# Other scratch tiles for the top-k masks, other banks and places for the index-query evictions, split first loads, and a later load of the last norm's scale, in a hybrid decoder layer

## The chip, the cores and the metric

One core of a Trainium2 chip. The time is that of one execution on the device, in microseconds. Engines are named as in the profile: PE (TensorE) with its weight loads PEld, DVE (VectorE), ACT (ScalarE), POOL (GpSimd) and SP (SyncE, which here only issues loads). The kernel before takes 1724.82 us (median of three runs, 1723.39 to 1730.63).

## The reference

One decoder layer for 1024 tokens of width 1024, all in float32:

```python
proj = x @ w_in                                  # 4696 columns: z, xbc, dt, q, k, v, qi, ki, wi
xbc  = silu(causal_conv4(xbc))                   # 1536 channels
y    = ssd_scan(xs, dt, a, bm, cm) + d_skip * xs # 16 heads x 64, 8 chunks of 128
y_ssd = rms_norm_by_group(y * silu(z)) * ssd_norm_g
ki   = layer_norm(ki)                            # one index key of 64 per token
score = sum_h wi_h * relu(qi_h . ki / 8)         # 8 index heads; causal
keys  = top_k(score, 256)                        # per query
y_att = softmax(q . k / 8 over keys) @ v         # 16 heads, 4 kv heads
h    = layer_norm(2**0.25 * x + [y_ssd, y_att] @ w_out)
u    = causal_conv3(h @ w_up)                    # 2 x 2816 columns
out  = layer_norm(2**0.25 * h + (silu(gate) * up) @ w_down)   # ln2_g, ln2_b
```

## The kernel before, in words

Matmuls run in a float32 form in which each operand is split into a high and a low part; `three` (lines 157 to 160) makes one product of three matmuls. A weight tile is loaded to `w_raw`, split by ACT or POOL to `w_hi` and by POOL or DVE to `w_lo`.

The work in order of the program: `x` is loaded in eight blocks of 128 tokens and turned by PE (`xtp`) to `xTh`, `xTl`, in two halves of 512 tokens; a small projection gives dt, the index key and its weights, and the key is normed on DVE (`kn`, `kih`, `kil`). Four index-query tiles follow (lines 441 to 453): each is two halves of 24 matmuls into a bank, and of each half ACT copies two quarters and DVE makes the two low parts. Then the scores of blocks 7 to 2, each the sum of eight heads (PE, a relu by ACT, an accumulation by DVE), are woven with the first projections. Blocks 0 and 1 need no search.

The search for each query's 256th largest score (`topk_gen`) sets one bit of a threshold in each of 32 rounds, by counts on DVE (blocks 6, 4, 3) and ACT (7, 5, 2). After it, `topk_gen` makes one mask for each of the six blocks, all on DVE: `eq`, `pen` and `cum` are its scratch tiles (lines 379 to 411). Beside the search and the masks runs the generator `main`: the convolutions (`conv_tile`, raw rows in `xbc`), the SSD scan of two head groups, chunk by chunk (`ssd_gen`), their gates (`gate_gen`), the projections of z, v and q, and the key loads of attention (`k_load`). Two steps of `topk_gen` go with five of `main`. Attention (`att_unit`), the output projection, the first norm, the up-projection, and the down-projection in seven products P1, P2, P6, P7, P4, P5, P3 follow. The last norm uses `g2`, `b2`, loaded as two broadcast rows (`ln_consts`).

What sets the order: a planner lays out each engine's instructions at build time, by a simulated time line, taking those that come first in the program first; `tc.high_priority(n)` moves an instruction n places ahead. SP keeps the order of the program. A load that has to wait for a buffer so holds up every load behind it. Each buffer belongs to a group with a number of buffers, and a tile waits until one of its group is free. Those of this change, in SBUF: `s2` 5 (2 KB a partition: parts of the scan and the gates, `eq`, and at the start `crow`), `wo` 8 (4 KB: blocks of `x`, then scores, convolved rows, `pen`, `cum`, and the attention keys `kh`, `kl`), `tx` 4 (4 KB: raw rows of the convolutions), `t4` 18, `wr` 3 (raw loads: weights, and the attention keys `kraw`); in PSUM: `ip` 2, `lg` 3, `tp` 2, `pv` 1 banks.

Of the kernel before, what the change touches and what calls it, by code (L numbers as in the profile page):

```python
# [8 lines left out]
F32 = mybir.dt.float32  # L9
F32R = mybir.dt.float32r  # L10
BF16 = mybir.dt.bfloat16
I32 = mybir.dt.int32
AF = mybir.ActivationFunctionType
OP = mybir.AluOpType
# [43 lines left out]
def hybrid_layer(ctx, tc, x, w_in, ssd_conv_w, ssd_conv_b, dt_bias, a_log, d_skip, ssd_norm_g,  # L58
# [30 lines left out]
    def f(t):  # L89
        return t.bitcast(F32)  # L90
# [3 lines left out]


    xb = [big("xload", tag="wo") for _ in range(NB)]
    for b in range(4):
        nc.sync.dma_start(xb[b], x[b * P:(b + 1) * P, :])

    ident = consts.tile([P, P], F32, name="ident")  # L100
    make_identity(nc, ident)
# [87 lines left out]
    nc.sync.dma_start(crow[0:48], bass.AP(tensor=ssd_conv_w.tensor, offset=ssd_conv_w.offset, ap=[[P, 48], [1, P]]))  # L189
    nc.sync.dma_start(crow[48:60], bass.AP(tensor=ssd_conv_b.tensor, offset=ssd_conv_b.offset, ap=[[P, 12], [1, P]]))  # L190
    nc.sync.dma_start(crow[60:68], bass.AP(tensor=ssd_norm_g.tensor, offset=ssd_norm_g.offset, ap=[[P, 8], [1, P]]))
    cw = consts.tile([P, 68], F32, name="cw")
    ps = bank("cwps", "tp")
    nc.tensor.transpose(ps[:, :68], crow[:68], ident[:68, :68])
    nc.scalar.activation(cw, ps[:, :68], AF.Copy)

    for half in range(2):
        s = slice(half * 512, half * 512 + 512)
        for k in range(NK):
# [122 lines left out]
    def topk_gen():  # L322
        thr, val, cand = [], [], []
        for e, ch in enumerate(CHAINS):
            thr.append(consts.tile([P, len(ch)], F32, name=f"thr{e}"))
            val.append(consts.tile([P, len(ch)], F32, name=f"val{e}"))
            for i, (b, eng) in enumerate(ch):
                nc.vector.memset(thr[e][:, i:i + 1], float((b + 1) * P - (TOPK if eng == "dve" else 2 * TOPK)))
            cand.append(small(f"cand{e}", (P, len(ch)), I32))
            nc.vector.memset(cand[e], 0)  # L330
        junk = big("junk", BF16, (P, 2, 1024))
        junk = [junk[:, 0], junk[:, 1]]
        top, at, tile16 = {}, 2048, None
        for b in [b for ch in CHAINS for b, eng in ch if eng == "dve"]:
            n = (b + 1) * P
            if tile16 is None:
                tile16, at = big("top16", BF16, (P, 2048)), 0
            if at + n > 2048:
                continue
            top[b] = tile16[:, at:at + n]  # L340
            at += n
            halves = score_ap[b].bitcast(BF16).rearrange("p (n t) -> p n t", t=2)
            nc.vector.tensor_copy(top[b], halves[:, :, 1])
        for k in range(31, -1, -1):
            for e, ch in enumerate(CHAINS):
                shape = (P, len(ch))
                for i, (b, eng) in enumerate(ch):
                    n = (b + 1) * P
                    c = f(cand[e][:, i:i + 1])
                    if eng == "dve":  # L350
                        nc.vector.tensor_scalar(junk[0][:, :n], top[b] if k >= 16 and b in top else score_ap[b], c, None,
                                                op0=OP.is_lt, op1=OP.add, accum_out=val[e][:, i:i + 1])
                    else:
                        nc.scalar.activation(junk[1][:, :n], score_ap[b], AF.Sign, bias=c, scale=-1.0,  # L354
                                             accum_out=val[e][:, i:i + 1])
                base = cand[e]
                if 0 < k < 31:
                    base = small(f"base{e}", shape, I32)
                    nc.vector.tensor_scalar(base, cand[e], 1 << (k - 1), None, op0=OP.bitwise_xor)
                fail = small(f"fail{e}", shape, I32)  # L360
                nc.vector.tensor_tensor(fail, val[e], thr[e], op=OP.is_gt)
                new = small(f"cand{e}", shape, I32)
                if k == 31:
                    neg = small(f"neg{e}", shape, I32, bufs=1)
                    nc.vector.tensor_scalar(neg, fail, 31, 31, op0=OP.logical_shift_left, op1=OP.arith_shift_right)
                    nc.vector.tensor_scalar(new, neg, 1 << 30, None, op0=OP.bitwise_xor)
                else:
                    nc.vector.scalar_tensor_tensor(new, fail, k, base, op0=OP.logical_shift_left, op1=OP.bitwise_xor)  # L368
                cand[e] = new
            yield  # L370
        m76 = big("mask76", BF16, (P, 2048))
        m5 = big("mask542", BF16, (P, 2048))
        m3 = consts.tile([P, 512], BF16, name="mask3")
        mask_ap[7], mask_ap[6] = m76[:, :1024], m76[:, 1024:1920]
        mask_ap[5], mask_ap[4], mask_ap[2] = m5[:, :768], m5[:, 768:1408], m5[:, 1408:1792]
        mask_ap[3] = m3[:, :512]
        zero = consts.tile([P, 1], F32, name="zero1")
        nc.vector.memset(zero, 0.0)
        for e, ch in enumerate(CHAINS):
            for i, (b, eng) in enumerate(ch):  # L380
                n = (b + 1) * P
                sc = score_ap[b]
                v = f(cand[e][:, i:i + 1])
                eq = mid("eq", BF16, (P, 1024))
                if eng == "act":
                    t = v
                    cnt = small("cnt", (P, 3))
                    nc.vector.tensor_scalar(eq[:, :n], sc, t, None, op0=OP.is_gt, op1=OP.add,
                                            accum_out=cnt[:, 0:1])
                    pen = big("pen", tag="wo")  # L390
                    nc.vector.tensor_scalar(pen[:, :n], sc, t, 3.0e38, op0=OP.is_le, op1=OP.mult)
                    nc.vector.tensor_tensor_reduce(pen[:, :n], sc, pen[:, :n], 1.0, 3.0e38, OP.add, OP.min,
                                                   cnt[:, 1:2])
                    nc.vector.tensor_scalar(cnt[:, 2:3], cnt[:, 0:1], float(TOPK), None, op0=OP.is_ge)
                    nc.vector.tensor_scalar(cnt[:, 2:3], cnt[:, 2:3], 6.0e38 / 2, None, op0=OP.mult)
                    nc.vector.tensor_scalar(cnt[:, 0:1], cnt[:, 0:1], float(TOPK) - 0.5, None, op0=OP.is_lt)
                    nc.vector.tensor_scalar(cnt[:, 0:1], cnt[:, 0:1], -3.0e38, None, op0=OP.mult)
                    nc.vector.tensor_tensor(cnt[:, 2:3], cnt[:, 2:3], cnt[:, 0:1], op=OP.add)
                    v = small("vsel", (P, 1))
                    nc.vector.tensor_tensor(v, cnt[:, 1:2], cnt[:, 2:3], op=OP.min)  # L400
                    nc.vector.tensor_tensor(v, v, t, op=OP.max)
                    yield
                room = small("room", (P, 2))
                nc.vector.tensor_scalar(eq[:, :n], sc, v, None, op0=OP.is_gt, op1=OP.add, accum_out=room[:, 0:1])
                nc.vector.tensor_scalar(room[:, 1:2], room[:, 0:1], float(TOPK), -BIG, op0=OP.subtract, op1=OP.mult)
                nc.vector.tensor_scalar(eq[:, :n], sc, v, BIG, op0=OP.is_equal, op1=OP.mult)
                cum = big("cum", tag="wo")
                nc.vector.tensor_tensor_scan(cum[:, :n], eq[:, :n], zero.to_broadcast([P, n]), 0.0, OP.add, OP.add)
                nc.vector.scalar_tensor_tensor(eq[:, :n], cum[:, :n], room[:, 1:2], eq[:, :n], op0=OP.is_le, op1=OP.mult)
                nc.vector.tensor_scalar(eq[:, :n], eq[:, :n], -1.0, BIG, op0=OP.mult, op1=OP.add)  # L410
                nc.vector.scalar_tensor_tensor(mask_ap[b], sc, v, eq[:, :n], op0=OP.is_le, op1=OP.mult)
                yield
# [30 lines left out]
    for t in range(4):  # L443
        w = w_qi if t == 0 else next_w()
        a, c = big("qsa", F32R, tag="pp"), big("qsb", F32R, tag="pp")
        for half in range(2):
            s = slice(half * 512, half * 512 + 512)
            ps = cols_half(w, xt, half)
            nc.scalar.activation(a[:64, s], ps[:64], AF.Copy)
            nc.scalar.activation(c[64:, s], ps[64:], AF.Copy)  # L450
            nc.vector.tensor_tensor(a[64:, s], ps[:64], f(a[:64, s]), op=OP.subtract)
            nc.vector.tensor_tensor(c[:64, s], ps[64:], f(c[64:, s]), op=OP.subtract)  # L452
        qs += [a, c]


    def qk_tile(dst, t, halves=(0, 1), w=None):
# [632 lines left out]


    KT = NF // 2
    g2, b2 = ln_consts(ln2_g, ln2_b)

    def two(src, r0, step, c0, n, width, k, tag):

        m = min(2, KT - k)
# [115 lines left out]
        now(nc.scalar.activation, c1[t], pa[t], AF.Copy)  # L1212
    r1 = h_rows(0)
    run("P2", pa, True)
    for t in range(4):
        now(nc.vector.scalar_tensor_tensor, r1[t][:, N1], r1[t][:, N1], ALPHA, pa[t], op0=OP.mult, op1=OP.add)
        stats(st8[t], 0, r1[t])
# [53 lines left out]
```

## Time and profile before

| what | value |
|---|---|
| median of 3 runs | 1724.82 us |
| profiled execution | 1727.09 us, its span 1725.4 us |
| mean granted PE clock | 0.963 |
| busy PE / DVE / ACT / POOL | 1598.4 / 1212.8 / 921.4 / 873.9 us |
| moved by DMA | 232.86 MB, 135 GB/s in the mean |

The span runs from the first to the last instruction of the profiled execution. Busy time counts an engine's instructions; of PE it says nothing of its clock, which is told as a share of full speed: 1.00 is 2.4 GHz, 0.50 is 1.2 GHz, and a value between them is a stretch with both.

### The profile page before, as it was taken

The page shows a single profiled execution, that of the slowest core. Times are in us where ns is not written, and L with a number is a line of the kernel's source. Part 1 is how long each engine was busy: PE and PEld are TensorE (multiplying, and loading weights), DVE is VectorE, ACT ScalarE, POOL GpSimd, SP SyncE. Part 2 cuts the span into 40 slices and gives each one's busy share as a digit, 9 for nine tenths or more (in the row PEclk, how much of TensorE's full clock was granted, in tenths as well). Part 3 has the DMA queues.
Part 4 walks back from the last instruction along what each step waited for, and adds up shares of the span by engine and source line. Part 5 has one row for each costly group of instructions (what it writes and reads, how often), then busy time and mean ns, then how long its engine had stood idle before and what let it go on. Part 6 is the DMA issues. An engine that isn't in the chain of part 4 may idle for free.

```text
span 1725.4 us, 23252 instructions
## 1 busy us (share of the span) xinstructions
PE 1598.4 (93%) x7844; PEld 1322.7 (77%) x7844; DVE 1212.8 (70%) x2274; ACT 921.4 (53%) x1761; POOL 873.9 (51%) x659
## 2 busy tenths in 40 slices
PE   8899998987998779999999893999999999989997
PEld 6688887776888657778888772878888888768886
DVE  3533779899369377787787479677777678746468
ACT  3333597687642376666676444555555555442241
POOL 2222235544264353545474456667777676565480
PEclk9999998999999989999999996999999999989999
DMA  5122022132433473544454542233444333788782
GB/s 170 41 78 68 25 95 77 50 103 69 129 99 92 135 227 100 153 138 139 130 157 157 159 155 77 86 116 131 144 132 143 116 116 110 242 318 300 233 280 110
DMA packets 208271, 232.86 MB, mean 135 GB/s; under 512 B 13987, under 2 KB 138263, under 8 KB 208151
## 3 DMA queue, kind: packets, MB, share of 16 engines
q1 hardware_dynamic: 160423, 159.79, 30.9%
q10 hardware_dynamic: 47728, 71.58, 11.4%
q8 instruction: 62, 1.02, 0.3%
q14 instruction: 58, 0.48, 0.1%
HBM read 159.70 MB, written 71.63 MB: 134 GB/s over the span
## 4 chain that ended last, share of the span: by engine, by line
PE 52%; DVE 6%; DMA 2%; ACT 2%; issue 1%; POOL 1%; ACTq 0%; DVEq 0%; SPq 0%; POOLq 0%
PE acc L158 4%; PE acc L159 4%; PE acc L160 4%; PE ops L158 3%; PE ops L159 3%; PE ops L160 3%; PE ptp L690 3%; PE pa L158 2%; PE pa L160 2%; PE pa L159 2%; PE pc L160 2%; PE pc L158 2%; PE pc L159 2%; PE pd L158 2%; PE pd L160 2%; PE pd L159 2%
## 5 line engine op out<-in xcount | busy, mean ns | idle before, releaser
L158 PE MATMUL proj<-xTh,w_hi 128*128 128x512 f32 (+1 forms) x432 | 174.5, 404 | 17.3 <-DVE qsb L452 6.3
L160 PE MATMUL proj<-xTh,w_lo 128*128 128x512 f32 (+1 forms) x432 | 172.9, 401 | 2.8 <-POOL w_lo L131 2.8
L159 PE MATMUL proj<-xTl,w_hi 128*128 128x512 f32 (+1 forms) x432 | 174.6, 404 | 0.0
L684 POOL TENSOR_SCALAR prob<-prob,sm 128x512 f32<-128x512 f32 (+7 forms) x128 | 97.0, 768 | 138.4 <-DVE sm L683 108.2
L997 POOL TENSOR_TENSOR w_hl<-s,w_hl 128x512 fp32r<-128x512 f32 x88 | 120.0, 1371 | 58.2 <-ACT w_hl L996 54.2
L128 POOL TENSOR_SCALAR w_hi<-w_raw 128x1024 fp32r<-128x1024 f32 x35 | 39.6, 1133 | 172.2 <-PE proj L159 125.3
L131 POOL TENSOR_TENSOR w_lo<-w_raw,w_hi 128x1024 fp32r<-128x1024 f32 (+1 forms) x45 | 113.3, 2521 | 26.1 <-ACT w_hi L130 23.9
L159 PE MATMUL acc<-wd_hl,g_hl 128*128 128x512 f32 x308 | 121.1, 395 | 0.4 <-POOL wd_hl L1158 0.4
L160 PE MATMUL acc<-wd_hl,g_hl 128*128 128x512 f32 x308 | 120.9, 394 | 0.0
L997 POOL TENSOR_TENSOR w_hl<-w_raw,w_hl 128x512 fp32r<-128x512 f32 x66 | 91.0, 1381 | 58.7 <-ACT w_hl L996 56.6
L158 PE MATMUL acc<-wd_hl,g_hl 128*128 128x512 f32 x308 | 110.9, 395 | 9.2 <-ACT wd_hl L1157 9.2
L681 ACT ACTIVATE prob<-prob,mx 128x512 f32<-128x512 f32 (+7 forms) x128 | 98.5, 771 | 36.5 <-DVE mx L678 36.3
L692 ACT ACTIVATE pt<-ptp 128x512 fp32r<-128x512 f32 x144 | 81.1, 595 | 64.6 <-PE ptp L690 43.9
L158 PEld LDWEIGHTS proj<-xTh,w_hi 128*128 128x128 f32 (+1 forms) x432 | 82.8, 192 | 37.5 <-issue 7.1
L1158 POOL TENSOR_TENSOR wd_hl<-keep,wd_hl 128x512 fp32r<-128x512 f32 x55 | 82.5, 1526 | 53.5 <-ACT wd_hl L1157 47.0
L158 PE MATMUL ops<-w_hi,y_hi 128*128 128x512 f32 x256 | 104.5, 408 | 3.1 <-ACT y_hi L130 3.1
L693 DVE TENSOR_TENSOR pt<-ptp,pt 128x512 fp32r<-128x512 f32 x144 | 95.4, 684 | 15.4 <-ACT pt L692 15.1
L159 PE MATMUL ops<-w_lo,y_hi 128*128 128x512 f32 x256 | 102.9, 402 | 0.4 <-DVE w_lo L131 0.4
L354 ACT ACTIVATE junk<-score,cand 128x1024 bf16<-128x1024 f32 (+2 forms) x96 | 86.0, 895 | 32.1 <-DVE cand L368 30.5
L160 PE MATMUL ops<-w_hi,y_lo 128*128 128x512 f32 x256 | 101.4, 399 | 0.0
L158 PE MATMUL tps<-w_hi,xTh 128*128 128x256 f32 x320 | 95.4, 299 | 3.6 <-ACT tout L612 2.1
L160 PEld LDWEIGHTS proj<-xTh,w_lo 128*128 128x128 f32 (+1 forms) x432 | 82.7, 192 | 20.0 <-POOL w_lo L131 3.2
(346 smaller groups left out, 5001.2 us busy)
## 6 DMA issues: line engine op xcount, KB each, us to landing
w_raw<-in_ffn_w_up_dram SPq DMA_DIRECT2D x44, 512.0 KB, 3.9
g_hl<-gs_dr SPq DMA_DIRECT2D x44, 512.0 KB, 5.4
w_raw<-in_w_in_dram SPq DMA_DIRECT2D x36, 512.0 KB, 3.9
r_dr<-rout ACTq DMA_DIRECT2D x48, 256.0 KB, 2.1
g_dr<-gt ACTq DMA_DIRECT2D x33, 256.0 KB, 3.4
keep<-in_ffn_w_down_dram SPq DMA_DIRECT2D x33, 256.0 KB, 5.7
acsb<-a_dr SPq DMA_DIRECT2D x16, 512.0 KB, 4.0
w_raw<-in_w_out_dram SPq DMA_DIRECT2D x16, 512.0 KB, 4.4
```

The source lines that it names most:

```text
L131: (nc.vector if lo_on_dve else nc.gpsimd).tensor_tensor(lo, raw, f(hi), op=OP.subtract)
L158: nc.tensor.matmul(ps, ah, bh, start=start, stop=False, skip_group_check=onto)
L159: nc.tensor.matmul(ps, ah, bl, start=False, stop=False, skip_group_check=onto)
L160: nc.tensor.matmul(ps, al, bh, start=False, stop=stop, skip_group_check=onto)
L354: nc.scalar.activation(junk[1][:, :n], score_ap[b], AF.Sign, bias=c, scale=-1.0, accum_out=val[e][:, i:i + 1])
L681: nc.scalar.activation(t[:, :w], t[:, :w], AF.Exp, bias=mx[:, h:h + 1], scale=-1.0, accum_out=sm[:, h:h + 1])
L684: nc.gpsimd.tensor_scalar(t[:, :w], t[:, :w], sm[:, 4 + h:5 + h], 1.0, op0=OP.mult, op1=OP.mult)
L690: nc.tensor.transpose(ps[:, h * P:(h + 1) * P], pr[h][:, kt * P:(kt + 1) * P], ident)
L692: nc.scalar.activation(pt[:, 0], ps, AF.Copy)
L693: nc.vector.tensor_tensor(pt[:, 1], ps, f(pt[:, 0]), op=OP.subtract)
L997: nc.gpsimd.tensor_tensor(t[:, 1], src, f(t[:, 0]), op=OP.subtract)
L1158: nc.gpsimd.tensor_tensor(wt[:, 1], w_raw, f(wt[:, 0]), op=OP.subtract)
```

## The change

Five edits. The first four blocks of `x` are loaded in eight pieces, the left halves first. The transpose of the convolution weights (`cw`) stands behind the index queries instead of ahead of the transposes of `x`. The scratch tiles of the masks come from `tx`. The index queries use banks of `ip` and `lg` by turns, and their evictions have a priority of 300. The load of `g2`, `b2` stands behind product P2 instead of ahead of P1.

```diff
     xb = [big("xload", tag="wo") for _ in range(NB)]
-    for b in range(4):
-        nc.sync.dma_start(xb[b], x[b * P:(b + 1) * P, :])
+    for n in range(2):
+        for b in range(4):
+            nc.sync.dma_start(xb[b][:, n * 512:n * 512 + 512], x[b * P:(b + 1) * P, n * 512:n * 512 + 512])
...
-    cw = consts.tile([P, 68], F32, name="cw")
-    ps = bank("cwps", "tp")
-    nc.tensor.transpose(ps[:, :68], crow[:68], ident[:68, :68])
-    nc.scalar.activation(cw, ps[:, :68], AF.Copy)
-
     for half in range(2):
...
                 v = f(cand[e][:, i:i + 1])
-                eq = mid("eq", BF16, (P, 1024))
+                eq = big("eq", BF16, (P, 1024), "tx")
...
-                    pen = big("pen", tag="wo")
+                    pen = big("pen", tag="tx")
...
-                cum = big("cum", tag="wo")
+                cum = big("cum", tag="tx")
...
-            ps = cols_half(w, xt, half)
-            nc.scalar.activation(a[:64, s], ps[:64], AF.Copy)
-            nc.scalar.activation(c[64:, s], ps[64:], AF.Copy)
-            nc.vector.tensor_tensor(a[64:, s], ps[:64], f(a[:64, s]), op=OP.subtract)
-            nc.vector.tensor_tensor(c[:64, s], ps[64:], f(c[64:, s]), op=OP.subtract)
+            ps = cols_half(w, xt, half, ("ip", "lg")[t % 2])
+            with tc.high_priority(EV_PRIO):
+                nc.scalar.activation(a[:64, s], ps[:64], AF.Copy)
+                nc.scalar.activation(c[64:, s], ps[64:], AF.Copy)
+                nc.vector.tensor_tensor(a[64:, s], ps[:64], f(a[:64, s]), op=OP.subtract)
+                nc.vector.tensor_tensor(c[:64, s], ps[64:], f(c[64:, s]), op=OP.subtract)
         qs += [a, c]
+
+    cw = consts.tile([P, 68], F32, name="cw")
+    ps = bank("cwps", "tp")
+    nc.tensor.transpose(ps[:, :68], crow[:68], ident[:68, :68])
+    nc.scalar.activation(cw, ps[:, :68], AF.Copy)
...
     KT = NF // 2
-    g2, b2 = ln_consts(ln2_g, ln2_b)
-
...
     run("P2", pa, True)
+    g2, b2 = ln_consts(ln2_g, ln2_b)
     for t in range(4):
```

## Rows read from the trace of the kernel before

**Rows 1.** The page: busy us, share of the span and instructions of PE.
```profile
PE 1598.4 (93%) x7844; PEld 1322.7 (77%) x7844; DVE 1212.8 (70%) x2274; ACT 921.4 (53%) x1761; POOL 873.9 (51%) x659
```
**Rows 2.** Time line, 43 to 51 us: start, duration, engine, line, what; idle time before.
```profile
43.53 3.64 DVE L237 TENSOR_SCALAR kn<-tok,mv,rs 128x64 f32<-128x64 f32 x3
...
49.21 0.69 DVE L452 TENSOR_TENSOR qsb<-proj,qsb 64x512 fp32r<-64x512 f32 x1
...
50.05 0.76 PE L158 MATMUL proj<-xTh,w_hi 128*128 128x512 f32 x1 [6.31 <-DVE qsb L452]
```
**Rows 3.** Busy time by stretch, 50 to 54 us: length, PE, PEld, DVE, ACT, POOL, PEclk.
```profile
50.00:54.00 4.00, 3.95 (x9) 3.13 (x10) 3.86 (x9) 0.00 (x0) 0.00 (x0) 0.50 0.00 0
```
**Rows 4.** Time line of DVE, 434 to 572 us: thresholds and masks.
```profile
434.56 0.15 DVE L368 SCALAR_TENSOR_TENSOR cand<-fail,cand 128x4 int32<-128x4 int32 x1
...
446.51 0.76 DVE L391 TENSOR_SCALAR pen<-score,cand 128x1024 f32<-128x1024 f32 x1 [2.53 <-PE xsp L495]
...
502.95 1.28 DVE L388 TENSOR_SCALAR_CACHE_REDUCE eq<-score,cand 128x1024 bf16<-128x1024 f32 x1
...
570.86 0.75 DVE L411 SCALAR_TENSOR_TENSOR mask<-score,cand,eq 128x512 bf16<-128x512 f32 x1
```
**Rows 5.** Busy time by stretch, 480 to 640 us, columns as in rows 3.
```profile
480.00:500.00 20.00, 20.00 (x157) 18.56 (x156) 9.24 (x9) 10.38 (x24) 17.51 (x14) 1.00 0.63 171
...
520.00:540.00 20.00, 16.21 (x136) 16.00 (x134) 19.93 (x34) 2.98 (x6) 11.11 (x6) 0.97 0.35 95
540.00:560.00 20.00, 19.27 (x108) 16.10 (x109) 18.04 (x32) 6.44 (x14) 7.65 (x7) 0.86 0.30 87
560.00:580.00 20.00, 15.59 (x76) 12.51 (x75) 12.04 (x15) 4.91 (x8) 11.76 (x9) 0.99 0.30 89
580.00:600.00 20.00, 18.13 (x67) 13.98 (x68) 4.15 (x6) 8.80 (x20) 3.25 (x2) 0.84 0.62 197
600.00:620.00 20.00, 12.96 (x43) 9.15 (x42) 11.00 (x14) 12.00 (x18) 4.76 (x2) 0.66 0.60 159
620.00:640.00 20.00, 15.62 (x79) 12.04 (x77) 15.69 (x57) 17.26 (x41) 11.06 (x9) 0.91 0.84 248
```
**Rows 6.** Waits, 420 to 640 us: total us, times, longest; the last two SP's own.
```profile
ACT kh L639 <- DVE eq L409: 7.6, 2, 7.2
...
SPq L139 <- DVE eq L410: 17.4, 1, 17.4
...
SPq L570 <- DVE mask L411: 13.7, 1, 13.7
```
**Rows 7.** Time line of SP, 533 to 541 us.
```profile
533.88 5.74 SPq L637 DMA_DIRECT2D kraw<-k_dr  x4
539.68 0.58 SPq L520 DMA_DIRECT2D acsb<-a_dr  x1
```
**Rows 8.** Time line of the start, 0 to 23 us.
```profile
0.81 1.83 SPq L98 DMA_DIRECT2D xload<-in_x_dram  x4
...
4.82 0.88 PE L202 MATMUL xtp<-ident,xload 128*128 128x128 f32 x3 [4.82 <-DMA xload<-in_x_dram]
...
9.16 0.90 PE L202 MATMUL xtp<-ident,xload 128*128 128x128 f32 x3 [0.52 <-DMA xload<-in_x_dram]
...
9.68 1.58 ACT L204 ACTIVATE xTh<-xtp 128x512 fp32r<-128x512 f32 x3 [7.60 <-PE xtp L202]
...
22.13 0.25 PE L194 MATMUL cwps<-ident,crow 68*128 68x68 f32 x1 [0.31 <-DMA crow<-in_ssd_conv_w_dram]
```
**Rows 9.** The tile `xbc`: durations in ns (min/median/max), first and last start in us.
```profile
L476 ACT ACTIVATE xbc<-proj x24: 574/586/600, 165.7 to 452.7; 128x512 f32<-128x512 f32 x24
```
**Rows 10.** The tile `kh`, in the same form.
```profile
L675 PE MATMUL lgps<-kh,qst x192: 276/366/775, 620.9 to 952.9; 128*128 128x512 f32 x48, 128*128 128x384 f32 x48, 128*128 128x256 f32 x32, 128*128 128x448 f32 x32
```
**Rows 11.** Time line of SP at 1471 us.
```profile
1471.40 0.34 SPq L749 DMA_DIRECT2D ln_g<-in_ln_g_dram  x1
```
**Rows 12.** Busy time by stretch, 1560 to 1600 us, with DMA share and GB/s.
```profile
1560.00:1600.00 40.00, 40.00 (x178) 33.12 (x177) 27.51 (x35) 9.81 (x16) 22.88 (x16) 1.00 0.87 294
```

## The prediction, made before the result was known

> **What bounds the kernel now.** I read the page first, then the busy time by stretch, then the waits and the order of time wherever TensorE was not full. The page gives PE 1598.4 of 1725.4 us [rows 1], so an edit can only win where PE stands still or runs at the lower clock. Two such places belong to edits of this change.
>
> The first ends at 50 us. PE waits 6.31 us for DVE's eviction `qsb` (line 452), which stood behind the `kn` instructions of the key norm [rows 2]: the second query tile wants a bank of the pair `ip`, and both still hold the first one. For the next four us PE works at a granted clock of 0.50, the lower of its two levels [rows 3].
>
> The second is the stretch from 520 to 640 us. The last bit of the thresholds is set at 434.56, so the masks could start then. One instruction of theirs does run at 446.51 (`pen`, whose tile is of the group `wo`). The first `eq`, which stands ahead of it in the program, runs at 502.95, and the last mask is written at 570.86 [rows 4]. DVE is busy for 9.24 us of the 20 from 480 to 500 [rows 5], so it isn't DVE that keeps `eq` back. What differs is the tile: `eq` comes from the group `s2`, five buffers which the SSD scan of group 1 refills all this time. I take the missing `s2` buffer as the cause. Late masks hold `wo` (scores, `cum`): `kh` waits 7.6 us on a mask's `eq`, and SP, whose queue keeps the order of the program, waits 17.4 us for `eq` at line 139 and 13.7 us for a mask at line 570 [rows 6]. Behind `kraw` loads that start at 533.88 stands the `acsb` load of a scan chunk, issued at 539.68 [rows 7]. This is where PE loses time.
>
> In between, the top-k search runs on DVE and ACT; it follows the scores, and these follow PE, so what PE gains at the start should move all of it.
>
> **The parts, step by step.** Terms are against the profiled execution, 1727.09 us (span 1725.4 and 1.7 around it). The median of the runs shown is 1724.82, 2.3 lower.
>
> *Query evictions.* Odd tiles go to a bank of `lg` (three), even ones to `ip`, and the four evictions of each half get a 300 better place. The second tile no longer needs the first one's banks, so the 6.3 us go whether or not the evictions come earlier. With the idle time goes the slow stretch behind it: 3.95 us busy at half clock [rows 3], half of that, 2.0. Term: -8.3. What is late next: eight evictions of 0.69 us [rows 2] may go ahead of the key norm, 5.5 us. PE covers them, since it then has three tiles of 48 matmuls; nine took 4 us at half clock [rows 3], so 0.22 us each at full, 32 us. Without that cover the 5.5 would come back. Bounds: -8.3 to 0.
>
> *First loads in halves.* SP issues four loads in 1.83 us, 0.46 each; PE turns the first block at 4.82, the fourth at 9.16, 1.45 apart, and the first `xTh` is made at 9.68 [rows 8]. Now the first four loads carry the left half of all four blocks. At 0.72 each the first lands at 4.1 and the fourth at 6.3, 2.9 us earlier. Against it: four more issues, 1.8 us, ahead of the loads of `w_small`, of the first query weight and of blocks 4 to 7. Bounds -2.9 to +1.8; I take -1.5, nearer to the gain, because PE has the transposes of this half to do while the weights come.
>
> *`cw` later.* The transpose had a wait of 0.31 us on a load [rows 8]; it now stands behind the queries, before any convolution uses it. Term -0.3; bounds -0.6 to +0.3. `crow` keeps an `s2` buffer longer, while nobody else wants one.
>
> *Scratch in `tx`.* `tx` (four buffers) holds the raw rows of the convolutions; the last is evicted at 452.7 [rows 9], and none is made in the last stage. So `eq`, `pen` and `cum` find tiles from about 435 on, the masks move up by some 60 us into a DVE that is half idle, `wo` comes free for `kh`, and SP's queue moves. The same DVE instructions run as before, none is added. Price: the PE time lost in the stretch, idle time plus busy time times what is missing of the clock [rows 5]. From 520 to 600: 3.8 + 0.7 + 4.4 + 1.9 idle, and 0.5 + 2.7 + 0.2 + 2.9 of clock: 17.1 us. From 600 to 640: 7.0 + 4.4 idle and 4.4 + 1.4 of clock: 17.2 us. The first sum is where the waits on masks lie, and I take it whole. The second is the hand-over to attention (first logits at 620.9 [rows 10]), where the output weights, the queries and the gate of group 1 come at once; part of it comes from the late gate, but I take none. Term -17.1. Bounds: 0 (attention starts as late for another reason) to -34.3; the other sign is the last rival.
>
> *`g2`, `b2` later.* Two loads of 512 KB leave SP's queue from 1471.40 on [rows 11] and now come behind the loads of product P2. At 1471 they held up nobody I can find; later they fall among loads at a DMA share of 0.87, beside a PE that is full for all 40 us [rows 12]. Their 1 MB is 3.6 us at the 294 GB/s of that row, and the operands are loaded ahead in eight buffers (`pp`), so 0. If that cover fails, +3.6; if SP was short of time at 1471, -1.
>
> Sum: -8.3 - 1.5 - 0.3 - 17.1 + 0 = -27.2; 1727.1 - 27.2 = 1699.9, and by the median's distance 1697.6, so **1698 us**.
>
> **Rivals.**
> *Only the start counts* (18 in 100). The masks come early, but the attention start is set by the last query projections and their way through DRAM, or PE's order is dealt anew and loses elsewhere. For it: the 17.2 us from 600 to 640 show more than one cause. Against: the waits that name `eq` and a mask. 1727.1 - 10.1 - 2.3 = 1714.7.
>
> *The hand-over shrinks too* (12). The gate of group 1 follows the scan; if it ends as much earlier as the masks, output weights and queries don't collide with it. 1727.1 - 10.1 - 34.3 - 2.3 = 1680.4.
>
> *It doesn't do what it says* (8). The planner still puts the masks behind the scan, which has the better priority (100), and the search swallows the early gain, being bound by its own chain. Only loads and `cw` remain: 1727.1 - 1.8 - 2.3 = 1723.0.
>
> *The halves land no faster than whole blocks* (4). If each of the eight loads takes the 1.45 us of a block, the last columns are there at 4.82 + 7 x 1.45 = 15.0 instead of 9.16: 5.8 us later, and the 1.5 are not won. 1697.6 + 7.3 = 1704.9. Against it: in 4.34 us three blocks, 1.5 MB, land [rows 8], so loads in flight together overlap. The Trainium skill, "DMA: Bandwidth & Descriptors" (Anatomy of one DMA, Rules for kernel authors), speaks for it: it gives a transfer a fixed part of some 2.0 us and asks for 1 MiB or more in each, by which four more transfers in single file would cost an estimated 8 us.
>
> *Slower: the masks starve the last convolution* (6). From 434.6 on, masks and conv tile 7 want the same four `tx` buffers. If freed ones pass from mask to mask, tile 7 can't be evicted, its bank stays taken, and PE stands. A mask takes (571.6 - 503.0) / 6 = 11.4 us [rows 4]; after four of them it is 480, not 452.7: 27.5 us of wait and 2.0 of low clock, and the scan that needs this tile starts as much later, which eats the gain behind it. 1727.1 - 10.1 + 29.5 - 2.3 = 1744. It decides from a wait of 10 us. Against it: at 435 one or two raw tiles live, and the convolution stands earlier in the program.
>
> **How the numbers follow.** The forecast has 52 in 100; its own range is 1690 to 1708 (loads and `g2` at their bounds, the mask term between 10 and 24). The range of 1682 to 1717 takes in "only the start", the halves and most of the shrinking hand-over; outside lie the slower case, "doesn't do" and the tail of the large gain. A measurement can tell about 0.5%, 8.6 us, from no change. Faster: 52 + 4 + 12 and 14 of the 18, 82; same: the other 4 and 8, 12; slower: 6.
>
> **What would show it.** No PE gap near 44 us and clock 1.00 there; the first `xTh` at about 7 us; the first `eq` at about 430 and the last mask before 510; `kh` before 515; `acsb` loads without the late one; first logits at 590 to 597. Wrong would be: `eq` still after 480 (no lack of `s2`), early masks and first logits after 605 (another cause holds attention), or a PE gap between 430 and 480 (`tx` starved).

## The result, and the profile after

The changed kernel takes 1704.18 us (median of 4 runs, 1701.0 to 1706.58) beside 1724.11 us for the kernel before on the same chip: a ratio of 0.9876, 95% interval 0.9856 to 0.9896. By this ratio, which is worked out from all the runs, that is 21.4 us less (the two medians alone lie 19.9 apart); the forecast was 1698 us, 27.2 less. The profiled execution took 1701.0 us, its span is 1699.1.

On the page, PE's busy time is 8.4 us shorter, with the same 7844 instructions [rows 1]; the rest of the 26.3 us of span was idle time.

```profile
PE 1590.0 (94%) x7844; PEld 1319.0 (78%) x7844; DVE 1218.1 (72%) x2274; ACT 917.5 (54%) x1759; POOL 882.0 (52%) x659
```

The start of the changed kernel, in order of time: the transposes wait for the left halves until 6.98 us, where they waited for blocks until 9.16; the first `xTh` is 2.2 us earlier [rows 8].

```profile
3.56 0.87 PE L198 MATMUL xtp<-ident,xload 128*128 128x128 f32 x3 [3.56 <-DMA xload<-in_x_dram]
...
6.98 0.91 PE L198 MATMUL xtp<-ident,xload 128*128 128x128 f32 x3 [0.50 <-DMA xload<-in_x_dram]
7.49 1.58 ACT L200 ACTIVATE xTh<-xtp 128x512 fp32r<-128x512 f32 x3 [5.41 <-PE xtp L198]
```

Its busy time from 50 to 54 us: PE runs at a granted clock of 1.00 (of 0.50 before [rows 3]), and the gap of 6.31 us ahead of it is gone [rows 2].

```profile
50.00:54.00 4.00, 4.00 (x20) 3.30 (x19) 3.92 (x5) 2.70 (x5) 3.92 (x3) 1.00 0.01 2
```

DVE from 423 to 506 us: the last threshold bit comes 10.8 us earlier, the first `eq` 67.9 us, the last mask 67.0 us [rows 4].

```profile
423.77 0.16 DVE L364 SCALAR_TENSOR_TENSOR cand<-fail,cand 128x4 int32<-128x4 int32 x1
435.04 1.27 DVE L384 TENSOR_SCALAR_CACHE_REDUCE eq<-score,cand 128x1024 bf16<-128x1024 f32 x1
...
503.87 1.57 DVE L407 SCALAR_TENSOR_TENSOR mask<-score,cand,eq 128x512 bf16<-128x512 f32 x1
```

Busy time by stretch (columns as in [rows 3] and [rows 12]), first the kernel before, from 440 to 520 us, then the changed one. Lost time of PE is length less busy time times clock.

```profile
440.00:520.00 80.00, 77.91 (x578) 71.38 (x577) 43.11 (x55) 42.93 (x103) 37.31 (x30) 1.00 0.40 117
```
```profile
440.00:520.00 80.00, 70.69 (x500) 63.85 (x500) 74.56 (x103) 42.22 (x100) 38.30 (x27) 0.94 0.42 120
520.00:600.00 80.00, 77.64 (x463) 68.05 (x463) 31.07 (x36) 33.78 (x66) 38.98 (x26) 0.98 0.50 145
600.00:640.00 40.00, 32.44 (x170) 24.84 (x169) 26.96 (x91) 27.99 (x58) 17.13 (x18) 0.96 0.57 177
```

From 520 to 600 us PE loses 3.9 us instead of 17.1, from 600 to 640 8.9 instead of 17.2 [rows 5]. But from 440 to 520 it loses 13.6 where it lost 2.1: DVE is busy for 74.56 of these 80 us, and PE's two longest waits in them are for steps of the SSD scan on DVE. The changed kernel's PE in order of time:

```profile
474.74 3.68 PE L561 MATMUL yps<-xdt,lmat 128*128 128x64 f32 x16 [2.49 <-DVE lmat L533]
497.33 1.34 PE L545 MATMUL yoff<-state,conv 128*128 128x512 f32 x2 [4.46 <-DVE state L555]
```

The tiles `kh` and `xbc`, and SP's queue, in the changed kernel: the last `kh` is made at 523.7 (569.8 before), the late `acsb` load goes out at 519.86, 19.8 us earlier [rows 7], the waits of SP for `eq` and a mask [rows 6] are gone, and attention's first logits run at 600.1, 20.8 us earlier [rows 10].

```profile
L641 ACT ACTIVATE kh<-kraw x4: 1057/1058/1062, 497.3 to 523.7; 128x1024 fp32r<-128x1024 f32 x4
L677 PE MATMUL lgps<-kh,qst x192: 276/368/775, 600.1 to 937.0; 128*128 128x512 f32 x48, 128*128 128x384 f32 x48, 128*128 128x256 f32 x32, 128*128 128x448 f32 x32
...
L478 ACT ACTIVATE xbc<-proj x24: 573/592/631, 154.3 to 443.0; 128x512 f32<-128x512 f32 x24
```
```profile
507.26 12.49 SPq L639 DMA_DIRECT2D kraw<-k_dr  x4
519.86 0.53 SPq L522 DMA_DIRECT2D acsb<-a_dr  x1
```

By the last accumulation of the kernel the lead has grown to 26.0 us (1715.5 to 1689.5). Its second part arises at the start of the down-projection: the norm's loads now go out at 1518.20, and PE's one long wait there is 3.26 us.

```profile
1494.62 1.93 PE L159 MATMUL acc<-wd_hl,g_hl 128*128 128x512 f32 x4 [3.26 <-ACT wd_hl L1157]
```
```profile
1518.20 0.38 SPq L751 DMA_DIRECT2D ln_g<-in_ln_g_dram  x1
```

In the kernel before, the same place looks like this (PE in order of time, then busy time by stretch): 7.98 us of wait, and a DMA share of 0.99 around it.

```profile
1519.83 1.65 PE L158 MATMUL acc<-wd_hl,g_hl 128*128 128x512 f32 x3 [7.98 <-ACT wd_hl L1157]
```
```profile
1480.00:1500.00 20.00, 18.44 (x73) 14.42 (x73) 15.86 (x21) 11.30 (x19) 6.61 (x5) 0.91 0.53 172
1500.00:1520.00 20.00, 12.02 (x54) 9.65 (x53) 8.87 (x9) 5.43 (x10) 10.83 (x9) 0.88 0.99 367
1520.00:1540.00 20.00, 20.00 (x78) 16.28 (x79) 9.19 (x8) 11.11 (x22) 12.35 (x9) 0.87 0.83 295
```

### The profile page after: what moved, and what is told of

It is laid out like the page before. It is cut to its first block, busy times and chain, and to the rows that moved or that the text cites. A ratio compares the mean times of both kernels' runs of the same rounds, so it can differ in the third digit from the quotient of the medians.

```text
span 1699.1 us, 23245 instructions
## 1 busy us (share of the span) xinstructions
PE 1590.0 (94%) x7844; PEld 1319.0 (78%) x7844; DVE 1218.1 (72%) x2274; ACT 917.5 (54%) x1759; POOL 882.0 (52%) x659
## 3 DMA queue, kind: packets, MB, share of 16 engines
q8 instruction: 62, 1.02, 0.3%
## 4 chain that ended last, share of the span: by engine, by line
PE 47%; DVE 5%; DMA 2%; ACT 1%; issue 1%; POOL 0%; SPq 0%; ACTq 0%; DVEq 0%; POOLq 0%
PE acc L159 4%; PE acc L160 4%; PE acc L161 4%; PE pa L159 2%; PE pd L159 2%; PE pa L161 2%; PE pa L160 2%; PE pc L159 2%; PE pc L160 2%; PE pd L161 2%; PE pc L161 2%; PE pd L160 2%; PE ops L160 2%; PE ops L159 2%; PE ops L161 2%; PE ptp L692 2%
## 5 line engine op out<-in xcount | busy, mean ns | idle before, releaser
L129 POOL TENSOR_SCALAR w_hi<-w_raw 128x1024 fp32r<-128x1024 f32 x35 | 46.3, 1325 | 184.4 <-PE proj L160 124.4
```

Source lines behind the costliest of these rows:

```text
L129: nc.gpsimd.tensor_scalar(hi, raw, 1.0, 1.0, op0=OP.mult, op1=OP.mult)
```

## The experiments

All were timed beside the kernel before; ratios with 95% intervals. The other columns are from one profile of each kernel, in us: the last threshold bit, the last mask, the first logits, the last accumulation. They scatter: in the seven profiles with the start unchanged (before, e1, e3, e5, e6, eq_only, pencum_only) the last threshold bit comes between 429.8 and 434.6.

| kernel | ratio | threshold | mask | logits | last acc |
|---|---|---|---|---|---|
| before | 1 | 434.6 | 570.9 | 620.9 | 1715.5 |
| whole change | 0.9876 (0.9856 to 0.9896) | 423.8 | 503.9 | 600.1 | 1689.5 |
| e1_masks | 0.9917 (0.9899 to 0.9934) | 429.8 | 504.7 | 597.5 | 1700.3 |
| e2_queries | 0.9990 (0.9979 to 1.0001) | 430.5 | 567.7 | 616.2 | 1714.2 |
| e3_norm | 0.9949 (0.9929 to 0.9969) | 433.5 | 569.3 | 618.0 | 1705.7 |
| e4_loads | 1.0011 (0.9996 to 1.0026) | 434.2 | 571.9 | 621.7 | 1723.2 |
| e5_norm_wait | 1.0031 (1.0018 to 1.0044) | 433.5 | 570.3 | 619.4 | 1715.4 |
| e6_masks_norm | 0.9882 (0.9862 to 0.9902) | 433.9 | 508.8 | 601.8 | 1696.7 |
| eq_only | 0.9957 (0.9942 to 0.9972) | 432.0 | 533.9 | 609.9 | 1707.1 |
| pencum_only | 0.9998 (0.9984 to 1.0013) | 432.5 | 568.3 | 616.1 | 1714.0 |
| g_tp | 0.9898 (0.9880 to 0.9915) | 433.7 | 508.8 | 605.5 | 1696.2 |
| f_rows | 0.9867 (0.9851 to 0.9882) | 425.1 | 505.2 | 600.4 | 1694.1 |
| g_tp_rows | 0.9892 (0.9874 to 0.9910) | 434.0 | 510.6 | 607.9 | 1700.6 |
| h_whole | 0.9885 (0.9865 to 0.9905) | 432.8 | 507.3 | 606.6 | 1695.6 |

**One part alone.** Each of the four edits by itself on the kernel before.

*e1_masks*

```diff
-                eq = mid("eq", BF16, (P, 1024))
+                eq = big("eq", BF16, (P, 1024), "tx")
-                    pen = big("pen", tag="wo")
+                    pen = big("pen", tag="tx")
-                cum = big("cum", tag="wo")
+                cum = big("cum", tag="tx")
```

> The kernel before with nothing changed but the tiles of eq, pen and cum (group tx). Theory (the missing s2 buffer held the masks back, late masks cost TensorE time before attention): first eq right behind the last threshold, at 435 us (503 before), last mask near 515; first logits about 10 us earlier than before, at 611, because that is what the whole change gained in that stretch; time 1724.1 - 10 = 1714 (ratio 0.994). Prediction's own term: -17.1, 1707 (0.990). Rival (the masks moved but attention's start came earlier only because the search ended 10.8 us earlier): first logits within 2 us of 620.9, ratio 1.000.

14.3 us less (0.0083 of the 1727.28 us of the kernel before, timed beside it), between the two sizes that were expected; the rival is out. Its busy time by stretch:

```profile
440.00:520.00 80.00, 70.77 (x514) 64.55 (x513) 74.47 (x114) 40.60 (x94) 43.71 (x26) 0.98 0.37 116
520.00:600.00 80.00, 78.11 (x470) 67.53 (x469) 31.65 (x36) 33.47 (x64) 40.89 (x28) 1.00 0.49 147
600.00:640.00 40.00, 34.62 (x169) 26.34 (x170) 28.83 (x102) 31.51 (x70) 19.29 (x20) 0.91 0.55 171
```

PE loses 10.6, 1.9 and 8.5 us, against 2.1, 17.1 and 17.2 before: +8.5 - 15.2 - 8.7 = -15.4. What was forecast for 520 to 600 came, the hand-over to attention gave half of its loss as well, and a new loss from 440 to 520, where masks and scan share DVE, took that back.

*e2_queries*

```diff
-            ps = cols_half(w, xt, half)
-            nc.scalar.activation(a[:64, s], ps[:64], AF.Copy)
...
+            ps = cols_half(w, xt, half, ("ip", "lg")[t % 2])
+            with tc.high_priority(EV_PRIO):
+                nc.scalar.activation(a[:64, s], ps[:64], AF.Copy)
...
```

> The kernel before with nothing changed but the bank pairs and the priority of the indexer query evictions. Theory: no TensorE gap of 6.3 us near 44 us, the search ends 8 us earlier (last candidate at 426 instead of 434.6), and all later milestones follow: first logits 613, ratio 0.995. Rival (late masks swallow it: eq stays in s2, which the scan gives free at a time of its own): the search ends 8 us earlier, but first eq stays at 500 to 503 and first logits at 618 to 621, ratio 0.999 to 1.000.

1.7 us less, just inside the noise. The gap near 44 us is gone, but the search ends only 4.1 us earlier, which is within the scatter, and the first `eq` stays at 499.8. That is nearest to the rival, though the 8 us of both texts did not come and the first logits (616.2) lie between them. Busy time from 0 to the last score matmul, of the kernel before, the changed one and this one:

```profile
0.00:219.80 219.80, 205.03 (x942) 169.27 (x943) 105.17 (x149) 88.86 (x162) 60.88 (x47) 0.98 0.26 77
```
```profile
0.00:216.50 216.50, 209.90 (x974) 173.52 (x975) 107.95 (x152) 89.84 (x168) 68.01 (x47) 1.00 0.27 78
```
```profile
0.00:219.50 219.50, 211.23 (x988) 175.45 (x989) 104.31 (x152) 87.63 (x162) 68.90 (x49) 1.00 0.26 77
```

PE's gain at the start went to other work: 988 matmuls up to the last score instead of 942, at 0.222 us each (20 us of full stretches hold 90) 10.2 us, so the scores end when they did before.

*e3_norm*

```diff
-    g2, b2 = ln_consts(ln2_g, ln2_b)
...
     run("P2", pa, True)
+    g2, b2 = ln_consts(ln2_g, ln2_b)
```

> The kernel before with nothing changed but the place of the loads of the last norm's scale and offset (behind product P2). Theory A (read from the trace of the whole change: the stretch from the last sum over positions to the last accumulation got 9.5 us shorter, and the weights of product P1 were there earlier): all up to 1470 us as before, last accumulation 8 to 9 us earlier than 1715.1, ratio 0.995. Prediction's term: 0 (-1 to +3.6), ratio 0.9995 to 1.002. Rival (the 9.5 us come from what reaches the end of the kernel in another order after the earlier edits): ratio 1.000, and the run with the norm's loads left in place shows the gain.

8.8 us less: theory A. Up to the down-projection little moved (its first matmul runs at 1491.6, at 1493.0 before); then PE's long wait shrinks to 2.71 us. PE in order of time, then its busy time by stretch:

```profile
1510.84 2.08 PE L158 MATMUL acc<-wd_hl,g_hl 128*128 128x512 f32 x4 [2.71 <-ACT wd_hl L1155]
```
```profile
1480.00:1500.00 20.00, 20.00 (x90) 16.57 (x89) 16.23 (x24) 11.83 (x21) 8.31 (x6) 1.00 0.70 226
1500.00:1520.00 20.00, 17.29 (x70) 13.80 (x69) 10.22 (x8) 9.34 (x17) 15.92 (x11) 0.91 0.97 341
1520.00:1540.00 20.00, 20.00 (x90) 16.57 (x89) 13.93 (x9) 11.75 (x22) 16.11 (x11) 1.00 1.00 358
```

Lost time from 1480 to 1540 falls from 15.2 us (3.2 + 9.4 + 2.6) to 4.3: 6.8 us of idle time and 4.1 of low clock.

*e4_loads*

```diff
-    for b in range(4):
-        nc.sync.dma_start(xb[b], x[b * P:(b + 1) * P, :])
+    for n in range(2):
+        for b in range(4):
+            nc.sync.dma_start(xb[b][:, n * 512:n * 512 + 512], x[b * P:(b + 1) * P, n * 512:n * 512 + 512])
```

and `cw` behind the queries.

> The kernel before with the first loads of x in halves and the conv weights' transpose (cw) behind the queries, nothing else. Theory: first xTh at 7.5 us instead of 9.7, but the gap near 44 us takes the gain, since the second query tile waits there for DVE's key norm: search end within 1.5 us of 434.6, ratio 0.999 to 1.000. Prediction's terms: -1.8, ratio 0.999. Rival (halves land no faster): first xTh at 9.7 or later, ratio 1.000 to 1.003.

1.9 us more, with 1.0 inside the interval: alone the edit brings nothing, as the theory said. The first `xTh` comes at 8.7 instead of 9.7 us, the last one at 34.1 instead of 30.7.

**What the norm's loads cost: wait or bytes.**

*e5_norm_wait*

```diff
-    g2, b2 = ln_consts(ln2_g, ln2_b)
+    g2, b2 = big("ln_g"), big("ln_b")
+    nc.sync.dma_start(g2[:, :8], bcast_row(ln2_g, 8))
+    nc.sync.dma_start(b2[:, :8], bcast_row(ln2_b, 8))
...
     run("P2", pa, True)
+    nc.sync.dma_start(g2, bcast_row(ln2_g, D))
+    nc.sync.dma_start(b2, bcast_row(ln2_b, D))
```

> The kernel before; the last norm's two tiles are taken from group t4 at the old place, where only 8 columns of each are loaded (the issue still waits for the buffer), and the full 512 KB loads come behind product P2. It parts the bytes from the wait. Theory (the queue: in the kernel before, the issue of ln_g waits 24.3 us for a t4 buffer at the head of SP's queue, and the first raw<-g_dr load of product P1 behind it is issued at 1473.20 instead of 1451.30): the wait stays, last accumulation within 2.5 us of the kernel before's 1715.5, ratio 0.999 to 1.001. Rival (the 1 MB itself, in a stretch with a DMA share of 0.99): as with the loads moved whole, last accumulation near 1705.7, ratio 0.994 to 0.996.

By its time alone, 5.4 us more, the queue theory would look confirmed. The trace says the opposite. PE in order of time, and by stretch:

```profile
1511.71 1.20 PE L158 MATMUL acc<-wd_hl,g_hl 128*128 128x512 f32 x4 [3.58 <-ACT wd_hl L1159]
...
1569.00 0.79 PE L159 MATMUL acc<-wd_hl,g_hl 128*128 128x512 f32 x1 [4.59 <-POOL wd_hl L1160]
```
```profile
1480.00:1500.00 20.00, 19.47 (x85) 15.48 (x84) 16.55 (x23) 12.18 (x22) 8.91 (x6) 1.00 0.70 232
1500.00:1520.00 20.00, 16.25 (x63) 12.68 (x63) 9.77 (x10) 9.37 (x17) 15.32 (x12) 0.91 0.97 340
1520.00:1540.00 20.00, 20.00 (x90) 16.54 (x89) 11.97 (x9) 11.80 (x21) 14.06 (x10) 1.00 1.02 363
...
1560.00:1580.00 20.00, 15.22 (x55) 11.75 (x54) 16.24 (x19) 4.88 (x8) 16.22 (x8) 0.83 0.60 206
```

With the wait at the head of SP's queue kept and the 1 MB moved, the loss from 1480 to 1540 is 5.7 us. So 9.5 of the 10.9 us go with the two full loads, and not with the wait. A new loss of 7.4 us from 1560 to 1580 took most of it back: PE waits 4.59 us there for a weight conversion, and ACT's conversions wait for DVE, which had waited 6.3 us for PE just before. The traces of the other kernels have no loss there. Why the rest is slower still isn't settled; the profiled execution is the fastest of the twelve.

How the 1 MB costs so much is a question of its own, and it does not do so by filling the DMA at PE's wait. In the kernel before, the second of the two loads is issued at 1472.55 and is there 6.7 us later, long before that wait, and right ahead of the stretch at 0.99 the DMA all but stands still:

```profile
1492.00:1496.00 4.00, 2.66 (x7) 1.82 (x8) 4.00 (x6) 3.99 (x8) 3.02 (x3) 0.82 0.02 4
```

What differs is the order on ACT, which is laid down when a kernel is built. ACT in order of time, in the kernel before and in e5_norm_wait:

```profile
1489.82 1.48 ACT L1026 ACTIVATE v<-xu,fw 128x512 f32<-128x512 f32 x2 [3.90 <-DVE xu L1020]
1491.25 1.13 ACT L1151 ACTIVATE g_hl<-raw 128x512 fp32r<-128x512 f32 x2
```
```profile
1484.72 1.14 ACT L1153 ACTIVATE g_hl<-raw 128x512 fp32r<-128x512 f32 x2
1488.72 1.49 ACT L1026 ACTIVATE v<-xu,fw 128x512 f32<-128x512 f32 x2 [2.85 <-DVE xu L1020]
```

The first operand of product P1 (`g_hl`) is made behind a step of the convolution (`v`) that waits 3.90 us in the one, and ahead of that step in the other. SP needs the buffers of `raw` that come free with this work, and waits for them 9.6 and 4.8 us at the longest (1440 to 1560 us; total, times, longest):

```profile
SPq L1099 <- DVE g_hl L1152: 26.7, 7, 9.6
```
```profile
SPq L1101 <- DVE g_hl L1154: 18.5, 5, 4.8
```

The loads behind that wait come late and together, and that is the stretch at 0.99. The split holds in all traces: in the six kernels with the full loads at the old place `g_hl` stands behind `v`, and SP's longest wait of this kind up to 1520 us is 9.1 to 11.4 us; in the eight with them behind P2 it stands ahead, and the wait is 3.8 to 5.0. That the planner turns the order round because it counts the 1 MB on its simulated time line is likely, but not shown: a kernel with the loads at the old place and the conversions put ahead by hand was not run.

**What held the masks.**

*eq_only*: `eq` alone in `tx` (the first two lines of the diff of e1_masks). *pencum_only*: the other four.

> The kernel before with only eq in group tx; pen and cum stay in wo. Theory (eq waited for one of the five s2 buffers, nothing else held the masks): first eq at about 439, last mask before 515, ratio 0.990 to 0.994, as with all three tiles moved (0.9917). Rival (the masks need all three: cum finds no wo buffer, which scores and xload hold): first eq early, but the last mask after 540, ratio 0.996 to 1.000.

> The kernel before with only pen and cum in group tx; eq stays in s2. Theory (s2 is what keeps eq back): first eq at 495 to 505 as before, last mask 565 to 572, ratio 0.998 to 1.002. Rival (wo is the shortage that counts, for kh and the output weights behind it): eq as late, but attention's first logits 5 to 10 us earlier than 620.9, ratio 0.994 to 0.997.

The tile `eq` in eq_only and in pencum_only:

```profile
L388 DVE TENSOR_SCALAR_CACHE_REDUCE eq<-score,cand x3: 605/1007/1273, 441.0 to 466.2; 128x1024 bf16<-128x1024 f32 x1, 128x768 bf16<-128x768 f32 x1, 128x384 bf16<-128x384 f32 x1
```
```profile
L388 DVE TENSOR_SCALAR_CACHE_REDUCE eq<-score,cand x3: 601/995/1274, 501.5 to 535.0; 128x1024 bf16<-128x1024 f32 x1, 128x768 bf16<-128x768 f32 x1, 128x384 bf16<-128x384 f32 x1
```

Moving `eq` is what lets the masks begin (441.0 against 501.5), so the lack of an `s2` buffer is shown. It is worth 7.4 us. Moving `pen` and `cum` alone is worth nothing, but with `eq` moved it is worth the other 6.9 us: with `pen` and `cum` still in `wo`, the masks end at 533.9 instead of 504.7. Both texts for eq_only were half right; a shortage of `wo` stands behind that of `s2`. In pencum_only the first logits do come 4.8 us earlier (616.1), but nothing of it is left in the time.

**What the start is worth.**

*e6_masks_norm*: the edits of e1_masks and e3_norm together.

> The changed kernel without its edits at the start (queries, halves, cw): only scratch in tx and the norm's loads later. Theory (the product of the single edits, 0.9917 x 0.9949 = 0.987; the start's gain is used up in the search before 440 us): ratio 0.985 to 0.989, as the whole change (0.9876), and first logits near 598. Rival (prediction: the start is worth 10 us once the masks no longer hold attention back): ratio 0.993, 10 us more than the whole change, first logits near 610.

Without any edit at the start the ratio is 0.9882, that of the whole change 0.9876: the start is worth some 1 us, and at most some 6 by the intervals. The threshold ends 10.1 us later (433.9), the first logits only 1.7. Its busy time by stretch:

```profile
440.00:520.00 80.00, 70.78 (x507) 64.39 (x505) 75.65 (x114) 39.96 (x92) 39.63 (x23) 0.98 0.42 126
520.00:600.00 80.00, 79.62 (x486) 69.25 (x485) 34.20 (x39) 35.83 (x71) 41.94 (x30) 1.00 0.43 132
600.00:640.00 40.00, 32.50 (x162) 24.69 (x161) 24.04 (x81) 27.88 (x59) 20.98 (x19) 0.91 0.68 201
```

From 440 to 600 us it loses 11.0 us of PE time, the whole change 17.5: a PE that comes 10 us earlier loses 6.5 us more beside a DVE that is as full in both (75.65 and 74.56 of 80 us).

*g_tp, f_rows, g_tp_rows, h_whole.* On the changed kernel, g_tp takes another pair of banks, f_rows loads the residual rows later, g_tp_rows does both, and h_whole is f_rows with the first loads whole and `cw` early again.

```diff
-            ps = cols_half(w, xt, half, ("ip", "lg")[t % 2])
+            ps = cols_half(w, xt, half, ("ip", "tp")[t % 2])
```
```diff
-    r1 = h_rows(0)
     run("P2", pa, True)
+    r1 = h_rows(0)
```

> The changed kernel; odd query tiles take a bank of tp instead of lg. Theory (the start's gain is lost since the queries sit in the lg banks that the scores need: TensorE gets 32 more matmuls of other work ahead of the last score matmul, 974 against 942, 0.222 us each = 7.1 of the 10 us): here 43 fewer than in the changed kernel stand ahead of it, 43 x 0.222 = 9.5 us; last score matmul near 207 (216.5), search start near 213 (222.8), search end 6 to 9 us before 423.8, time 4 to 9 us below the changed kernel's 1704.2, ratio to before 0.982 to 0.985. Rival (the search's end is set by its own chain beside the convolutions, so nothing before 220 us counts): search start earlier, but last candidate and first logits within 3 us of 423.8 and 600.1, ratio 0.987 to 0.989.

Missed. 931 matmuls stand ahead of the last score, as counted, but the wait for DVE's eviction is back, and with it the threshold at 433.7:

```profile
48.48 0.77 PE L159 MATMUL proj<-xTh,w_hi 128*128 128x512 f32 x1 [6.16 <-DVE qsb L449]
```
```profile
0.00:218.70 218.70, 203.94 (x931) 167.30 (x932) 104.33 (x151) 85.07 (x159) 62.85 (x47) 0.98 0.27 79
```

So another pair of banks doesn't close the gap by itself: with `lg`, PE's order has other work there (251 matmuls in the first 60 us of the changed kernel, 211 here). The run doesn't decide the question it was made for; it does show once more that with the gap open the time is, within the intervals, that of e6_masks_norm.

> The changed kernel; the four loads of residual rows r1 (2 MB) are issued behind product P2 too. Theory (bytes: what is loaded at the P1/P2 transition delays P1's and P2's weights, at a DMA share near 1): the remaining wait of 3.26 us with its slow clock near 1494 (4.8 us of TensorE time) goes, last accumulation 3 to 5 us earlier than 1689.5, ratio to before 0.984 to 0.986. Rival (that wait comes from SP's queue or a buffer): wait stays, ratio 0.987 to 0.989.

PE's wait at this place falls from 3.26 to 1.90 us, and the time by 1.5 us of the 3 to 5 expected, less than can be told apart.

```profile
1498.71 0.50 PE L160 MATMUL acc<-wd_hl,g_hl 128*128 128x512 f32 x1 [1.90 <-POOL wd_hl L1158]
```

> Both edits of g_tp and f_rows on the changed kernel. Theory: the gains lie in different stretches and add, 8 to 13 us below the changed kernel, ratio to before 0.979 to 0.983. Rival (either is given back later): no better than the better one of the two.

> The kernel of f_rows (the changed kernel with the residual rows r1 loaded behind P2) with the first loads whole again and cw at its old place. Theory A (single edits add: the loads alone gave a ratio of 1.0011): 1 to 2 us faster than f_rows, ratio to before 0.984 to 0.986. Theory B (what stands ahead of the scores on TensorE decides what the start is worth: 988 matmuls up to the last score matmul as with the query edit alone, against 974 in the changed kernel, 14 x 0.222 = 3.1 us, and first xTh 2 us later): last score matmul near 221, search end 427 to 430 instead of 425.1, ratio 0.986 to 0.989, of which attention's start shows little (first logits 600 to 603, as in the kernel with masks and norm alone).

g_tp_rows is no better than the better of the two, as the rival said. h_whole has theory B's ratio: the last score matmul is at 219.6, and the threshold (432.8) and the first logits (606.6) are later than either text. None of these beats the changed kernel by more than the measurement can tell; f_rows (1703.96 us) is its equal.

## Why the prediction was right, and where it was not

The direction, the main mechanism and the range held (1704.2 in 1682 to 1717, and in the likeliest case's own 1690 to 1708). The sum hides two errors that nearly cancel: the start, sized at -10.1, brought about -1, and the norm's loads, sized at 0, brought -8.8. That the number came out so near is luck. The four single ratios multiply to 0.9867, so within the intervals the parts add, as the sum assumed.

**Query evictions, -8.3: -1.7 alone, not told from 0.** The first half of the step is right: gap and slow stretch are gone, and with the loads' edit PE loses 6.6 us in the first 60 instead of some 17. The second half, that what PE gains at the start moves all that follows, failed at two places. The last score came only 3.3 us earlier (216.5 for 219.8), since 32 more matmuls went ahead of it (7.1 us), and the search starts 2.8 us earlier (222.8 for 225.6). The search itself got shorter (197.7 us from DVE's first to its last count, 206.4 before), so the threshold did come 10.8 us earlier; that this is because the work done ahead was missing beside it is argued, not shown. From there on attention does not follow the search: e6_masks_norm has the threshold 10.1 us later and the logits 1.7. That DVE, with masks and scan at once, is what holds it then is argued from its 75 busy us of 80; a kernel with the scan's steps ahead of the masks was not run. The rival in which only the start counts is out: e6_masks_norm has the gain without it.

**Loads in halves and `cw`, -1.8: +1.9 alone, not told from 0.** The halves do land earlier, so the rival in which they land no faster, with the last columns at 15.0 us, is out: the last of the eight pieces was issued at 4.1 us, and no load of `x` took more than 6.1 to land. The Trainium skill's fixed part of some 2.0 us ("DMA: Bandwidth & Descriptors", Anatomy of one DMA) is given there for transfers that GpSimd issues, and SP issues these. It does not add up from piece to piece: the four left halves came 1.14 us apart (3.56 to 6.98). The gain was lost later.

**Scratch in `tx`, -17.1: -14.3 alone.** Right in cause and near in size, by three terms where I had one. The term from 520 to 600 came (-15.2). The hand-over, which I took at 0, gave 8.7 of its 17.2, so that rival was half true. And I had put the masks "into a DVE that is half idle" at no price: 9.24 of 20 us [rows 5] was the share with the scan alone, and the masks beside it filled DVE (74.47 of 80 us, 43.11 before), where 8.5 us were lost from 440 to 520. The slower rival, starved `tx` tiles, did not come: the last `xbc` is evicted at 443.0.

**`g2`, `b2` later, 0: -8.8, outside the bounds -1 to +3.6.** This step failed. I asked who waits for these loads, found nobody, and priced the place where they go. There they cost nothing, as forecast: in the changed kernel PE is full at a clock of 1.00 from 1500 to 1580. What counted was the old place. With the 1 MB there, ACT makes the first operands of P1 behind a step that waits 3.90 us, SP waits 9.6 us for the buffers that this frees, the loads behind it come together at a share of 0.99, and PE waits 7.98 us for weights. All these rows were in the trace of the kernel before. The lost time is more than the wait, since idle time came with a granted clock of 0.87 to 0.91 (4.1 of the 10.9 us).

**What would show it.** Gap, clock, first `xTh` (7.5), first `eq` (435.0) and last mask (503.9) came about as forecast. The last `kh` (523.7) missed 515, the late `acsb` load is still there, 20 us earlier, and the first logits (600.1) missed 590 to 597. Attention then gives some of it back: its last logits come 15.9 us earlier, not 20.8.

## What to carry to other kernels

When work is moved earlier into an engine that has room, add its busy time to what runs there, stretch by stretch: the room is gone when both come together, and what then waits is the chain that was using it. A gain is only worth what reaches the next place where engines meet; look for the milestone that several chains end at, and ask which of them is last. A load that nobody waits for can still have a price: read the waits of what is loaded behind it, and compare the order of each engine's instructions with and without it.

## What the runs showed of the hardware

Around the transition of the two products, the DMA moved 340 to 367 GB/s at shares of 0.97 to 1.02 in the stretches of 20 us shown above. More was seen in h_whole:

```profile
1520.00:1540.00 20.00, 20.00 (x89) 16.54 (x89) 8.01 (x8) 5.63 (x10) 7.82 (x7) 1.00 1.04 397
```

The Trainium skill, "DMA: Bandwidth & Descriptors" (Specifications), puts one core's half of what a memory stack gives at some 358 GB/s. The rows lie on both sides of that figure, and the 397 GB/s are 11% above it, so for this kernel, which runs on one core, it is no ceiling. Unexpected was what 1 MB can cost: moving it gave back 10.9 us of PE time, of which by an estimate only 2.9 us would be its transfer (1 MB at 367 GB/s). What the traces show behind the rest is another order on ACT, and a granted clock of 0.87 to 0.91 around the idle time.
